# Six layer norms over features: sums as columns of tokens and a root on 128x2, instead of sums and root on all partitions

## Chip, cores, metric

One core of a Trainium2 chip runs the whole program. The metric is device time in microseconds of one execution, over several runs.

## What is computed

Two layers of a diffusion backbone with 256 latent tokens and 256 context tokens of 1024 features. Each layer mixes tokens (long convolution, attention, pooling), projects, adds a residual and normalises; then a SwiGLU feed-forward follows, again with a residual and a norm. The norm is the part that this change is about:

```python
def layer_norm(x, g, b):
    xf = x.astype(jnp.float32)
    mu = jnp.mean(xf, axis=-1, keepdims=True)
    var = jnp.mean(jnp.square(xf - mu), axis=-1, keepdims=True)
    return ((xf - mu) * lax.rsqrt(var + EPS) * g + b).astype(x.dtype)
...
    xl = layer_norm(DN_ALPHA * xl + g1_l * stream_mixer(pl, ql, k_all, v_all, lp), lp['ln1_g'], lp['ln1_b'])
    xl = layer_norm(DN_ALPHA * xl + g2_l * swiglu(xl * (1 + sc2_l) + sh2_l, lp), lp['ln2_g'], lp['ln2_b'])

    if not last:
        qc = queries(pc, lp['q_norm_g'])
        xc = layer_norm(DN_ALPHA * xc + g1_c * stream_mixer(pc, qc, kc, vc, lp), lp['ln1_g'], lp['ln1_b'])
        xc = layer_norm(DN_ALPHA * xc + g2_c * swiglu(xc * (1 + sc2_c) + sh2_c, lp), lp['ln2_g'], lp['ln2_b'])
```

Layer 0 normalises both streams, latent and context, twice; layer 1 only the latent one. That makes six norms of 256 tokens each.

## The kernel before

Features lie on the partitions: x is 128 partitions by 8 tiles (KT) by tokens, 512 of them in layer 0 (stream 0 is the first 256, stream 1 the second) and 256 in layer 1. Weights are fetched in blocks of 128x1024 by DMAs on SP's queue (`wblock`), split by ACT into a rounded high part (`whi`, L162) and by DVE into the rest (`wlo`, L159), and every product is three matmuls on PE: high by high, high by low, low by high (L169, L170, L171; or L273 where `dense_by_feature` goes over the features in the outer loop, so that a feature tile of the input can be used as soon as it is there). Results of dense blocks go to three PSUM buffers (`mm`); norms and other small things share five more (`aux`). The tile framework gives every engine a list of instructions in an order that its scheduler sets from priorities; `high_priority` moves what stands in it ahead of other work. Each engine then takes its own list strictly in turn. Generators in `self.bg` are advanced a step at a time by `pump`, between tiles of a dense block.

A norm has four parts. `ln_start` (L867) takes a 128x512 buffer `lnacc`. `ln_tile` (L873, L879) is called for each of the eight feature tiles when its projection is in PSUM: L884 on DVE adds the gated projection to the residual in x (and so frees the PSUM buffer), L890 on ACT squares it into `lnq`, L894 and L895 add value and square to `lnacc`; the last tile's are left out of that. `ln_sums` (L897) multiplies `lnacc` with a 128x128 matrix of 1/1024, `self.ones`, which puts the sums over the 128 features of every token on all partitions of a PSUM tile, `lnbc` (L900). `ln_finish` (L902, L915) adds the last feature tile and its square to it in the same way (L922), so that `lnbc` holds mean and mean square of each token, the same on every partition. ACT squares the mean (L924), DVE makes the variance (L925) and a reciprocal root in two steps by `newton` (L286: L290, L297, L298, L300, L301) on 128x256, into `lnrm`; ACT copies the mean beside it (L927). Then, for feature tiles 0, 1 and pairs (2,3), (4,5), (6,7), DVE subtracts the mean (L932) and multiplies by the root (L933), and ACT and DVE make the next stage's operands (`h2` or `h`: L939, L944, L159) or the output (L947, L949, with an output DMA of each pair on SP, L1175).

What stands around the six norms:

- Layer 0, first norms. The last five tiles of the output projection `wo` are made for stream 0 and then, with the same five weight blocks, for stream 1 (L1144 to L1148). Stream 0's finish goes to `bg` and runs during stream 1's tiles. Behind them come the first blocks of the feed-forward, `f` (L169 on `h2h` for stream 0, L273 for stream 1).
- Layer 0, second norms. Both finishes give layer 1's input `h`; behind them come layer 1's first projections, `u` (three blocks by feature, L273) and `q`.
- Layer 1, first norm. Five blocks `f` are computed from the sum before it is normalised (`raw`, L273), and `from_raw` (L974: L977, L979, L980) corrects them with mean and root into `fraw`; the other blocks read the normalised `h` (L169).
- Layer 1, second norm: the end of the program.

Elsewhere, the column form exists already: `hfss` (L420) sums over partitions by matmuls with one column of `ones`, and `hfrs` takes the root on 128x2; `newton` has a branch for that shape (L294, one instruction for each column). `bcast_cols` (L317, L322, L323) multiplies the identity by a column on DVE and lets PE multiply that diagonal matrix by `ones`, which puts the column on all partitions as a row; it is used for the attention's keys (`krb`).

## Time and profile before

| | |
|---|---|
| median of three runs | 1701.2 us (1699.5 to 1703.41) |
| profiled execution | 1701.23 us |
| its span | 1699.4 us |
| granted TensorE clock, mean of the span | 0.993 |
| PE, PEld, DVE, ACT, POOL busy | 97%, 85%, 72%, 42%, 13% of the span |
| HBM | 141 GB/s over the span |

The span runs from the first instruction to the last. PE stands for matmuls, PEld for the loads of their stationary operand, which overlap with them. A busy share is an average over the program; the wait lists and timelines say what is late at one place.

### The profile page before, as it was taken

The numbers are of one execution on the slowest core, as the hardware profiler recorded it, in microseconds if no ns is written. First come the engines' busy times: TensorE is split into PE (matmuls) and PEld (weight loads), VectorE is DVE, ScalarE is ACT, GpSimd is POOL, SyncE is SP. The second block draws the span as 40 slices with busy tenths as digits, with TensorE's granted clock in tenths as the row PEclk, the third lists the DMA queues.
The fourth block names the chain that finished last, engine by engine and source line by source line (L and its number), as shares of the span: only waits on it lengthen the run. The fifth ranks groups of instructions, "written<-read, shape, count | busy, mean of one in ns | idle before, by whom it ended". The sixth has DMA issues, their size and how long they took to land.

```text
span 1699.4 us, 25553 instructions
## 1 busy us (share of the span) xinstructions
PE 1650.9 (97%) x9926; PEld 1443.3 (85%) x9926; DVE 1227.5 (72%) x2145; ACT 710.3 (42%) x1138; POOL 219.9 (13%) x169
## 2 busy tenths in 40 slices
PE   7999999999999999999999999999989899999996
PEld 1888878788888888988888888899989899989996
DVE  4688879755677775789876567498767986796655
ACT  2533332533454433442222222275425664564443
POOL 1134541000210000000000012113531100000000
PEclk9999999999999999999999999999999999999998
DMA  8422222453422344226666664144426435645552
GB/s 307 168 88 87 66 84 79 152 161 124 137 75 90 113 159 136 100 82 201 189 199 196 205 197 151 62 159 140 152 92 186 125 118 169 196 140 186 185 185 91
DMA packets 68897, 243.34 MB, mean 143 GB/s; under 512 B 8166, under 2 KB 8744, under 8 KB 68520
## 3 DMA queue, kind: packets, MB, share of 16 engines
q1 hardware_dynamic: 67192, 236.78, 42.8%
q0 software_dynamic: 1168, 4.72, 0.9%
q8 instruction: 78, 1.28, 0.3%
q10 hardware_dynamic: 416, 0.21, 0.1%
q14 instruction: 43, 0.35, 0.1%
HBM read 238.01 MB, written 1.05 MB: 141 GB/s over the span
## 4 chain that ended last, share of the span: by engine, by line
PE 84%; DVE 10%; ACT 3%; issue 2%; DMA 1%; POOL 0%; ACTq 0%; DVEq 0%; POOLq 0%
PE f L169 6%; PE f L171 6%; PE f L170 6%; PE g L169 4%; PE g L171 4%; PE g L170 4%; PE b L169 4%; PE b L171 4%; PE b L170 4%; PE w L169 4%; PE w L171 3%; PE w L170 3%; PE ux L169 2%; PE ux L170 2%; DVE wlo L159 2%
## 5 line engine op out<-in xcount | busy, mean ns | idle before, releaser
L162 ACT ACTIVATE whi<-raw 128x1024 fp32r<-128x1024 f32 x322 | 340.6, 1059 | 679.9 <-issue 203.6
L159 DVE TENSOR_TENSOR wlo<-raw,whi 128x1024 fp32r<-128x1024 f32 x310 | 402.9, 1301 | 199.4 <-ACT whi L162 196.6
L190 DVE SCALAR_TENSOR_TENSOR junk<-ada,silu 128x1024 bf16<-128x1024 f32 x128 | 158.7, 1241 | 39.3 <-DMA ada<-adat 38.5
L169 PE MATMUL f<-h2h,whi 128*128 128x512 f32 (+1 forms) x320 | 125.1, 391 | 0.1
L170 PE MATMUL f<-h2l,whi 128*128 128x512 f32 (+1 forms) x320 | 124.5, 389 | 0.0
L171 PE MATMUL f<-h2h,wlo 128*128 128x512 f32 (+1 forms) x320 | 124.5, 389 | 0.0
L169 PE MATMUL f<-h,whi 128*128 128x256 f32 x312 | 88.4, 283 | 1.7 <-DVE fraw L979 1.6
L169 PE MATMUL w<-a,whi 128*128 128x256 f32 (+1 forms) x284 | 90.1, 317 | 0.0
L170 PE MATMUL w<-a,whi 128*128 128x256 f32 (+1 forms) x284 | 89.3, 314 | 0.0
L171 PE MATMUL w<-a,wlo 128*128 128x256 f32 (+1 forms) x284 | 89.2, 314 | 0.0
L171 PE MATMUL f<-h,wlo 128*128 128x256 f32 x312 | 87.6, 281 | 0.6 <-DVE wlo L159 0.6
L170 PE MATMUL f<-h,whi 128*128 128x256 f32 x312 | 88.1, 282 | 0.0
L169 PE MATMUL g<-hh,whi 128*128 128x512 f32 x192 | 75.6, 394 | 0.0
L171 PE MATMUL g<-hh,wlo 128*128 128x512 f32 x192 | 75.4, 393 | 0.0
L170 PE MATMUL g<-hl,whi 128*128 128x512 f32 x192 | 75.3, 392 | 0.0
L169 PEld LDWEIGHTS f<-h2h,whi 128*128 128x128 f32 x320 | 60.0, 188 | 14.1 <-DVE sg L1022 0.9
L171 PEld LDWEIGHTS f<-h2h,wlo 128*128 128x128 f32 x320 | 60.1, 188 | 13.6
L170 PEld LDWEIGHTS f<-h2l,whi 128*128 128x128 f32 x320 | 60.1, 188 | 13.1
L169 PEld LDWEIGHTS f<-h,whi 128*128 128x128 f32 x312 | 58.4, 187 | 2.3 <-issue 1.9
L171 PEld LDWEIGHTS f<-h,wlo 128*128 128x128 f32 x312 | 59.2, 190 | 0.8 <-DVE wlo L159 0.8
L170 PEld LDWEIGHTS f<-h,whi 128*128 128x128 f32 x312 | 58.6, 188 | 0.0
L169 PEld LDWEIGHTS w<-a,whi 128*128 128x128 f32 x284 | 53.5, 188 | 3.9 <-issue 0.2
(483 smaller groups left out, 4789.1 us busy)
## 6 DMA issues: line engine op xcount, KB each, us to landing
raw<-wst SPq DMA_DIRECT2D x336, 512.0 KB, 3.5
ada<-adat SPq DMA_DIRECT2D x80, 512.0 KB, 3.8
adar<-ada SPq DMA_DIRECT2D x16, 512.0 KB, 9.5
x<-x_t POOLq DMA_DIRECT2D x1, 2048.0 KB, 9.7
x<-x_t SPq DMA_DIRECT2D x1, 1024.0 KB, 10.5
x<-x_t SPq DMA_DIRECT2D x2, 512.0 KB, 10.2
silu<-c_row SPq DMA_DIRECT2D x2, 512.0 KB, 7.4
wf<-hfw SPq DMA_DIRECT2D x4, 256.0 KB, 5.8
```

The source lines that it names most:

```text
L159: (eng or self.nc.vector).tensor_tensor(out=lo, in0=src, in1=hi.bitcast(F32), op=ALU.subtract)
L162: self.nc.scalar.activation(hi, src, AF.Copy)
L169: t.matmul(out, lhsT=ah, rhs=bh, start=start, stop=False)
L170: t.matmul(out, lhsT=ah, rhs=bl, start=False, stop=False)
L171: t.matmul(out, lhsT=al, rhs=bh, start=False, stop=stop)
L190: nc.vector.scalar_tensor_tensor(out=junk, in0=raw, scalar=1.0, in1=self.silu[:, s], op0=ALU.mult, op1=ALU.mult, accum_out=mod[:, s, m : m ...
```

## The change

The six norms get another form. In `ln_sums`, the tokens become the rows: `lnacc`, 128 tokens of it at a time, is the stationary operand and one column of `ones` the moving one, so each matmul gives the sums of 128 tokens as a column of 128 partitions (`lnst`, a PSUM tile of its own: two for the values, two for the squares); DVE copies these four columns (L902). In `ln_finish`, four more such matmuls give the last feature tile's sums (L908 for all eight), L930 adds the copy, and mean, variance and root are computed on 128x2 (L935, L936, `newton` with its branch for two columns). `bcast_cols` puts the mean, and after it the root, on all partitions, each by two diagonal matrices and two matmuls of 128 columns (L322, L323), into one PSUM tile `lnrb`; the diagonals are multiplied by 1024, since `ones` holds 1/1024. In layer 0 ACT copies both from PSUM to `lnrm` (L943); in layer 1 DVE reads them in PSUM (`keep`), and the first norm there makes the copies for `from_raw` as well. Subtraction and multiplication are L949 and L950. At the call for the first norm of each layer, the finish's priority `pf` goes from 0 to 100.

The diff:

```diff
--- before.py
+++ after.py
@@ -314,12 +314,12 @@
         nc.vector.tensor_scalar(out=a, in0=a, scalar1=PI_LO, scalar2=-PI_LO, op0=ALU.min, op1=ALU.max)
         nc.scalar.activation(out, a, AF.Sin)
 
-    def bcast_cols(self, ps_out, cols):
+    def bcast_cols(self, ps_out, cols, scale=1.0):
 
         nc = self.nc
         for i in range(cols.shape[1]):
             dg = self.sb.tile([P, P], F32, tag="diag", name=self.nm("diag"), bufs=2)
-            nc.vector.tensor_scalar_mul(dg, self.ident, cols[:, i : i + 1])
+            nc.vector.tensor_scalar(out=dg, in0=self.ident, scalar1=cols[:, i : i + 1], scalar2=float(scale), op0=ALU.mult, op1=ALU.mult)
             nc.tensor.matmul(ps_out[:, i * P : (i + 1) * P], lhsT=self.ones, rhs=dg, start=True, stop=True)
 
 
@@ -864,9 +864,9 @@
                 nc.vector.scalar_tensor_tensor(out=x, in0=x, scalar=scale, in1=cb, op0=ALU.mult, op1=ALU.subtract)
             yield
 
-    def ln_start(self, y, s, g, pt, pf):
+    def ln_start(self, y, s, g, pt, pf, keep):
         ts = slice(s * SEQ, (s + 1) * SEQ)
-        st = dict(y=y[:, :, ts], g=g[:, s], s=s, pt=pt, pf=pf)
+        st = dict(y=y[:, :, ts], g=g[:, s], s=s, pt=pt, pf=pf, keep=keep)
         st["acc"] = self.t2b(shape=[P, 2, SEQ], name="lnacc")
         return st
 
@@ -896,8 +896,16 @@
 
     def ln_sums(self, st):
 
-        bc = st["bc"] = self.aux([P, 2, SEQ], name="lnbc")
-        self.nc.tensor.matmul(bc, lhsT=self.ones, rhs=st["acc"], start=True, stop=False)
+        st["bc"] = self.aux(name="lnst")
+        self.ln_columns(st, (st["acc"][:, 0], st["acc"][:, 1]), 0)
+        st["c"] = self.small([P, 4], "lnc4")
+        self.nc.vector.tensor_copy(st["c"], st["bc"][:, 0:4])
+
+    def ln_columns(self, st, srcs, o):
+        for i, src in enumerate(srcs):
+            for j in range(2):
+                k = o + 2 * i + j
+                self.nc.tensor.matmul(st["bc"][:, k : k + 1], lhsT=src[:, j * P : (j + 1) * P], rhs=self.ones[:, 0:1], start=True, stop=True)
 
     def ln_finish(self, st, *a, **k):
         g = self.ln_finish_(st, *a, **k)
@@ -917,14 +925,23 @@
         nc = self.nc
         y, s = st["y"], st["s"]
         ts = slice(s * SEQ, (s + 1) * SEQ)
-        bc, a, t = st["bc"], st["acc"][:, 0], st["acc"][:, 1]
-        for i, src in enumerate((y[:, KT - 1], st["sq"])):
-            nc.tensor.matmul(bc[:, i], lhsT=self.ones, rhs=src, start=False, stop=i == 1)
-        rm = st["rm"] = self.t2b(shape=[P, 2, SEQ], name="lnrm")
-        nc.scalar.activation(t, bc[:, 0], AF.Square)
-        nc.vector.scalar_tensor_tensor(out=a, in0=bc[:, 1], scalar=EPS, in1=t, op0=ALU.add, op1=ALU.subtract)
-        self.newton(rm[:, 0], a, t)
-        nc.scalar.activation(rm[:, 1], bc[:, 0], AF.Copy)
+        self.ln_columns(st, (y[:, KT - 1], st["sq"]), 4)
+        c = st["c"]
+        nc.vector.tensor_tensor(out=c, in0=st["bc"][:, 4:8], in1=c, op=ALU.add)
+        rb = self.aux([P, 2, SEQ], name="lnrb")
+        self.bcast_cols(rb[:, 1], c[:, 0:2], D)
+        w = self.small([P, 4], "lnw")
+        a, t = w[:, 0:2], w[:, 2:4]
+        nc.vector.tensor_tensor(out=t, in0=c[:, 0:2], in1=c[:, 0:2], op=ALU.mult)
+        nc.vector.scalar_tensor_tensor(out=a, in0=c[:, 2:4], scalar=EPS, in1=t, op0=ALU.add, op1=ALU.subtract)
+        self.newton(c[:, 2:4], a, t)
+        self.bcast_cols(rb[:, 0], c[:, 2:4], D)
+        rm = rb
+        if "raw" in st or not st["keep"]:
+            st["rm"] = self.t2b(shape=[P, 2, SEQ], name="lnrm")
+            for i in (1, 0):
+                nc.scalar.activation(st["rm"][:, i], rb[:, i], AF.Copy)
+            rm = rb if st["keep"] else st["rm"]
         yield
         for i in range(0, KT, 2):
             for m, n in ((i, 1), (i + 1, 1)) if i == 0 else ((i, 2),):
@@ -1130,7 +1147,7 @@
         al = self.scaled(self.v(l, V_LN1G, 8), self.v(l, V_LN1B, 8))
         fo = [self.fold(self.v(l, V_LN1G, 8), self.v(l, V_LN1B, 8), mod[4][:, s], mod[3][:, s]) for s in range(ns)]
         raw = self.raw_pair(*fo[0]) if ns == 1 else None
-        lns = [self.ln_start(y, s, mod[2], (20, 50)[l], 0) for s in range(ns)]
+        lns = [self.ln_start(y, s, mod[2], (20, 50)[l], 100, last) for s in range(ns)]
         if raw:
             lns[0]["raw"] = raw, fo[0][0]
         for m in range(KT - nb):
@@ -1167,7 +1184,7 @@
         g, b = self.v(l, V_LN2G, 8), self.v(l, V_LN2B, 8)
 
         def start():
-            return [self.ln_start(y, s, mod[5], 0, (100, 0)[l]) for s in range(ns)]
+            return [self.ln_start(y, s, mod[5], 0, (100, 0)[l], last) for s in range(ns)]
 
         if last:
             def finish(s, st):
```

How the lists of instructions move is shown at two places. The names after L-number and operation are output, inputs and shape; `x` is the residual that becomes the normalised value, `h2l` and `h` the low part of the next stage's operand.

DVE, layer 0, first norms, before: the part of the list around L884 of stream 1's second `wo` tile (`wo_5878`).

```order
L925 SCALAR_TENSOR_TENSOR lnacc_5539<-lnbc_5811,lnacc_5539 128x256
L290 TENSOR_SCALAR lnrm_5866<-lnacc_5539 128x256
L297 TENSOR_TENSOR lnacc_5539<-lnrm_5866 128x256
L932 TENSOR_TENSOR x_4920<-x_4920,lnrm_5866 128x256
L298 TENSOR_TENSOR lnacc_5539<-lnacc_5539 128x256
L884 SCALAR_TENSOR_TENSOR x_4920<-wo_5878,mod_73,x_4920 128x256
L300 SCALAR_TENSOR_TENSOR lnacc_5539<-lnacc_5539 128x256
L894 TENSOR_TENSOR lnacc_5540<-lnacc_5540,x_4920 128x256
L301 SCALAR_TENSOR_TENSOR lnrm_5866<-lnacc_5539,lnrm_5866 128x256
L895 TENSOR_TENSOR lnacc_5540<-lnacc_5540,lnq_5904 128x256
L297 TENSOR_TENSOR lnacc_5539<-lnrm_5866 128x256
```

DVE at the same place in the change: from L930 to the same L884 (here `wo_5901`), in two pieces.

```order
L930 TENSOR_TENSOR lnc_1019_5816<-lnst_5811,lnc_1019_5816 128x4
L322 TENSOR_SCALAR diag_5875<-ident,lnc_1019_5816 128x128
L322 TENSOR_SCALAR diag_5878<-ident,lnc_1019_5816 128x128
L935 TENSOR_TENSOR lnw_5881<-lnc_1019_5816 128x2
L936 SCALAR_TENSOR_TENSOR lnw_5881<-lnc_1019_5816,lnw_5881 128x2
L290 TENSOR_SCALAR lnc_1019_5816<-lnw_5881 128x2
L294 SCALAR_TENSOR_TENSOR lnw_5881<-lnc_1019_5816,lnw_5881 128x1 x2
L300 SCALAR_TENSOR_TENSOR lnw_5881<-lnw_5881 128x2
L301 SCALAR_TENSOR_TENSOR lnc_1019_5816<-lnw_5881,lnc_1019_5816 128x2
L294 SCALAR_TENSOR_TENSOR lnw_5881<-lnc_1019_5816,lnw_5881 128x1 x2
L301 SCALAR_TENSOR_TENSOR lnc_1019_5816<-lnw_5881,lnc_1019_5816 128x2
```

```order
L159 TENSOR_TENSOR h2l_5659<-lnt_6016,h2h_5658 128x256
L961 TENSOR_SCALAR lnt_6020<-x_4920,fold_5531 128x256
L895 TENSOR_TENSOR lnacc_5540<-lnacc_5540,lnq_5865 128x256
L159 TENSOR_TENSOR h2l_5659<-lnt_6020,h2h_5658 128x256
L949 TENSOR_TENSOR x_4920<-x_4920,lnrm_5898 128x2x256
L884 SCALAR_TENSOR_TENSOR x_4920<-wo_5901,mod_73,x_4920 128x256
```

Before, this L884 is the fifth row behind L925. Now 33 rows of the list stand between L930 and it, three quarters of stream 0's finish among them.

DVE, second norm of layer 0, stream 0, before: the end of the root, and two splits of weights for `u` (`wlo_9104`, `wlo_9110`).

```order
L932 TENSOR_TENSOR x_4920<-x_4920,lnrm_8980 128x2x256
L298 TENSOR_TENSOR lnacc_7936<-lnacc_7936 128x256
L159 TENSOR_TENSOR wlo_9104<-raw_9101,whi_9103 128x1024
L301 SCALAR_TENSOR_TENSOR lnrm_8980<-lnacc_7936,lnrm_8980 128x256
L159 TENSOR_TENSOR wlo_9110<-raw_9107,whi_9109 128x1024
L933 SCALAR_TENSOR_TENSOR x_4920<-x_4920,lnrm_8980 128x256 x2
L944 TENSOR_SCALAR lnt_9009<-x_4920,fold_8959 128x256
```

DVE at the same place in the change: the first split of weights ahead of the subtraction, and the two others at the end of the norm (`u_9193` is the first product of `u` that DVE reads).

```order
L322 TENSOR_SCALAR diag_9052<-ident,lnc_1514_8986 128x128
L322 TENSOR_SCALAR diag_9055<-ident,lnc_1514_8986 128x128
L159 TENSOR_TENSOR wlo_9178<-raw_9175,whi_9177 128x1024
L949 TENSOR_TENSOR x_4920<-x_4920,lnrm_9058 128x256 x2
```

```order
L961 TENSOR_SCALAR lnt_9158<-x_4920,fold_9010 128x256
L159 TENSOR_TENSOR h_9009<-lnt_9154,h_9009 128x256
L159 TENSOR_TENSOR h_9009<-lnt_9158,h_9009 128x256
L159 TENSOR_TENSOR wlo_9184<-raw_9181,whi_9183 128x1024
L159 TENSOR_TENSOR wlo_9190<-raw_9187,whi_9189 128x1024
L547 SCALAR_TENSOR_TENSOR vv_9279<-u_9193,vecs,vv_9279 128x255
```

Two splits stood ahead of the first multiplication and the third behind the last `h`; now one stands ahead of it and two behind the last `h`. In PE's list, 46 rows of the second and third `u` products stand behind these two splits.

## Rows read from the trace of the kernel before

**Rows 1.** Page, part 1: busy time, share of the span, instructions of each engine.

```profile
PE 1650.9 (97%) x9926; PEld 1443.3 (85%) x9926; DVE 1227.5 (72%) x2145; ACT 710.3 (42%) x1138; POOL 219.9 (13%) x169
```

**Rows 2.** Waits of PE: us in total, times, longest us.

```profile
PE f L273 <- ACT h2h L939: 2.1, 1, 2.1
...
PE u L273 <- ACT h L939: 1.7, 1, 1.7
PE f L169 <- DVE fraw L979: 1.6, 1, 1.6
PE lnbc L900 <- DVE lnacc L895: 1.3, 1, 1.3
```

**Rows 3.** Timeline of PE: start us, duration us, engine, line, out<-in.

```profile
706.36 0.59 PE L922 MATMUL lnbc<-x,ones 128*128 128x256 f32 x2
...
707.33 0.28 PE L170 MATMUL wo<-mh,whi 128*128 128x256 f32 x1
707.45 0.28 PE L171 MATMUL wo<-mh,wlo 128*128 128x256 f32 x1
...
718.40 0.28 PE L169 MATMUL f<-h2h,wx 128*128 128x256 f32 x1
...
1121.76 0.28 PE L169 MATMUL q<-h,whi 128*128 128x256 f32 x1
```

**Rows 4.** Timeline, all engines: a column sum, then a root on 128x2.

```profile
76.71 0.40 PE L171 MATMUL ux<-hh,wlo 128*128 128x512 f32 x1
...
76.94 0.50 PE L420 MATMUL hfss<-ones,wf 128*128 128x1 f32 x4
...
77.48 0.16 DVE L423 TENSOR_SCALAR hfrs<-hfss 128x2 f32<-128x2 f32 x1 [2.33 <-PE hfss L420]
77.62 0.40 PE L170 MATMUL uv<-hl,whi 128*128 128x512 f32 x1
...
77.88 0.35 DVE L294 SCALAR_TENSOR_TENSOR hfrs<-hfrs 128x1 f32<-128x1 f32 x2
```

**Rows 5.** Timeline, all engines: diagonal matrices and their broadcast.

```profile
1245.68 0.51 DVE L322 TENSOR_SCALAR diag<-ident,krs 128x128 f32<-128x128 f32 x2 [0.45 <-PE krb L323]
...
1246.03 0.71 PE L323 MATMUL krb<-diag,ones 128*128 128x128 f32 x4
...
1246.70 0.28 PE L170 MATMUL v<-wlo,h 128*128 128x256 f32 x1
...
1246.78 0.69 DVE L710 SCALAR_TENSOR_TENSOR kf<-kf,krb 128x512 f32<-128x512 f32 x1 [0.58 <-PE krb L323]
```

**Rows 6.** Timeline of DVE, first norms of layer 0.

```profile
710.80 0.48 DVE L884 SCALAR_TENSOR_TENSOR x<-wo,mod,x 128x256 f32<-128x256 f32 x1
```

**Rows 7.** Timeline of DVE, second norm of layer 0, stream 0.

```profile
1109.20 0.75 DVE L933 SCALAR_TENSOR_TENSOR x<-x,lnrm 128x256 f32<-128x256 f32 x2
...
1110.86 0.69 DVE L933 SCALAR_TENSOR_TENSOR x<-x,lnrm 128x512 f32<-128x512 f32 x1
1111.46 0.42 DVE L159 TENSOR_TENSOR h<-lnt,h 128x256 fp32r<-128x256 f32 x1
...
1117.34 1.21 DVE L159 TENSOR_TENSOR wlo<-raw,whi 128x1024 fp32r<-128x1024 f32 x1
```

**Rows 8.** Stretch there: busy share of each engine, then PEclk, DMA share, GB/s.

```profile
1112.00:1115.00 3.00, 3.00 (x14) 3.00 (x15) 3.00 (x9) 3.00 (x7) 0.00 (x0) 0.50 0.77 292
```

**Rows 9.** Timeline of DVE, layer 1, first norm.

```profile
1491.58 0.42 DVE L925 SCALAR_TENSOR_TENSOR lnacc<-lnbc,lnacc 128x256 f32<-128x256 f32 x1
...
1500.01 0.76 DVE L933 SCALAR_TENSOR_TENSOR x<-x,lnrm 128x256 f32<-128x256 f32 x2
...
1506.46 0.86 DVE L979 SCALAR_TENSOR_TENSOR fraw<-lnrm,rawc,f 128x256 f32<-128x256 f32 x2
```

**Rows 10.** Timeline of DVE, last norm.

```profile
1686.45 0.42 DVE L925 SCALAR_TENSOR_TENSOR lnacc<-lnbc,lnacc 128x256 f32<-128x256 f32 x1 [1.72 <-ACT lnacc L924]
...
1692.30 1.96 DVE L933 SCALAR_TENSOR_TENSOR x<-x,lnrm 128x256 f32<-128x256 f32 x4
```


## The prediction

> **What bounds the kernel now.** I read the page first: PE is busy in 97% of the span [rows 1], so time is lost in two ways only, by giving PE more to do or by letting it stand. The next view is what PE waits for. At the six norms it stands 2.1 us before the by-feature matmuls of stream 1 of layer 0 (L273 on h2h), 1.7 us before the first matmul of layer 1 (L273 on h) and 1.6 us before the first dense block behind layer 1's first norm (L169 on fraw) [rows 2]. These are the places where a norm is the chain that ends last, with the end of the program as the fourth: behind the last norm there is no PE work left to cover it. The timelines of PE and DVE at these places give the prices, and the two order listings say what each queue holds behind what. The sum stands against the profiled execution, 1701.23 us (span 1699.4); the median of the three runs shown is 1701.2, so the two agree. A measurement of this kernel can tell about 0.2%, 3.4 us, from no change.
>
> **PE's work per norm.** Removed: one ones-matmul over 512 columns and two over 256. From 706.36 to 707.33 stand the two narrow ones and one wo matmul, whose pitch is 0.12 (707.33 to 707.45), so 0.85 [rows 3]. The wide one has as many columns as both: 1.7 in all. Added: eight matmuls with one column and four of 128 columns. Two single-column matmuls (four records) and one matmul of 512 columns, whose pitch is 0.23 (76.71 to 76.94), take 76.94 to 77.62, so 0.45 for two [rows 4]; eight make 1.8. Two broadcasts with a diagonal matrix (four records) and one v matmul of 0.12 lie between 1246.03 and 1246.70, so at most 0.55; I take 0.45, because that is the price of four such records in rows 4 and the load sets both [rows 5]. Four make 0.9. So **PE gets 2.7 in place of 1.7, +1.0 us a norm**; ends: +0.7 (if a wide ones-matmul costs 0.3 more than two narrow ones) and +1.2 (0.55 for each pair).
>
> **DVE's work per norm.** Removed: L925 and eight root steps on 128x256, with five subtractions 5.85 us from L925 to the first multiply in the last norm [rows 10]. The subtractions there are two of 256 and three of 512 columns. In a row, 256 columns take 0.34 (0.75 for two, less one of 0.42) and 512 take 0.60 (1110.86 to 1111.46) [rows 7], so 2.5 us, and the nine steps take 3.4. Added: a copy and an addition on 128x4, ten steps on 128x2, four diagonal matrices. Two steps go from 77.48 to 77.88, 0.20 each, and a pair of L294 with its hand-over takes 0.39 [rows 4]; ten make 2.0. Two diagonal matrices take 0.51, start to end [rows 5], about 0.4 to 0.5 in a row. Sum 3.4: DVE saves nothing. What changes is the shape. Before, the mean was on all partitions first and the five subtractions filled the gaps between root steps. Now mean and root share a PSUM tile, the first subtraction (L949) stands behind both pairs of diagonals in DVE's queue, and all subtractions are on the path behind the root.
>
> The price of 128x2 deserves a check. A step on 128x256 takes 0.42 [rows 10] and one on 128x2 takes 0.16 with a pitch of 0.20 [rows 4]: with 1/128 of the elements, more than a third of the time. [...] The trace's own 0.20 is what I use.
>
> **Chain from sums to first subtraction.** L930 0.2, two diagonals 0.4, L935 and L936 0.4, the root 1.65, two diagonals 0.4, and 0.6 from there to the reader (the idle 0.58 before L710 in rows 5): 3.65 us.
>
> **Layer 0, first norms: +2.9.** The change also raises the finish's priority from 0 to 100. In the after order all of stream 0's finish but its tail stands ahead of stream 1's L884 on its second wo tile, which runs at 710.80 now [rows 6] while the root is still being made. Between L930 and that L884 stand 4 diagonals (1.0), 10 small steps (2.0), 19 operations of 256 columns at 0.34 (6.5), 5 of 512 at 0.6 (3.0) and one weight split (1.2, as in rows 7): 13.7 us. From about 706, where the last sums are on PE now [rows 3], that ends at 719.7. Stream 1 has three mm buffers; its last wo tile needs the one that this L884 frees. PE would be there at 718.40 (first f matmul [rows 3]) less 24 matmuls of 0.12, plus 1.0: 716.5. It waits 3.2, and f starts at 722.6 and not 718.40. Then stream 1's own norm adds 1.0 less what the shorter queue behind it gives back (0.2), and its 2.1 us wait [rows 2] goes, since its finish then has more time: 4.2 + 0.8 - 2.1 = +2.9. Ends: 0 (the L884 slips in early enough) and +5.
>
> **Layer 0, second norms: +3.4.** The first multiply is at 1109.20 and PE's wait ends with it [rows 2, 7]. Now one weight split of 1.2 less stands ahead of it, and against that stand the columns, the two broadcasts' hand-overs and the subtractions: u starts within 0.3 of today. But the splits of the second and third u blocks stand behind all of h. One of them runs at 1117.34 now [rows 7], the other before the multiplies. In the after order, 46 PE rows stand behind them, at 0.12 a row 5.5 us. With h done at about 1117.4 and one split of 1.2 they can begin at 1118.6, so q starts at 1124.1 where it starts at 1121.76 [rows 3]: +2.3. Stream 1's broadcasts and hand-over add 1.1, since PE is full there. Ends: +1.1 (the splits get through) and +4.9 (half clock, below).
>
> **Layer 1, first norm: +2.8.** L925 runs at 1491.58, the first multiply, with all five subtractions done, at 1500.01, and fraw starts at 1506.46 [rows 9]. Now a weight split stands ahead of L930, so 1492.55; 3.65 for the chain and two splits of 1.2 inside it give the first subtraction at 1498.6. From there 2.5 for subtractions and the same 6.45 as today, plus up to 0.06 on each of ten operations that now read PSUM (L884, which does, takes 0.48 [rows 6], against 0.42): 1508.2, +1.8. The fourth dense block also waits for a buffer that the first fraw tiles free, behind copies (L994) that now stand together: +1 more, by the queue's rows. Ends: 0 (h's pieces come as early as now) and +4.3 (half clock).
>
> **Last norm: +0.5.** L925 starts at 1686.45 and waits for one activation behind the sums, so they are there at about 1686.0; plus 3.65 the first subtraction is at 1689.7; 2.5 of subtractions bring it to 1692.2, level with the 1692.30 of now [rows 10]. Ten operations that read PSUM cost 0.06 each more. Ends: -0.7 (first outputs leave earlier, and the last with them) and +1.
>
> **Sum:** 2.9 + 3.4 + 2.8 + 0.5 = +9.6 on 1701.2, so **1711**. PE's own +5 (five norms) is inside: where PE stands anyway it costs nothing. On ACT a square and a copy go and two copies come (layer 0): level. One early weight load moves later on SP's queue; the weights of that stretch are read many tiles later, so nothing, and a wait for it would show as PE on whi. A norm holds two PSUM aux buffers of five, not one; no wait for one is among rows 2, so nothing, at worst a tile's 0.5.
>
> **Rivals.**
> *Faster.* [...] 0.13.
> *Same.* The new waits fall on the old ones: stream 1's L884 is done by about 717, so that PE stands under 1 us there and the 2.1 goes (+0.5 in all), and both u splits are through by 1118 (only stream 1's +1.1 stays), and the fourth dense block's +1 is all that layer 1's first norm adds; with the last norm's +0.5 that is +3.1, 1704, and down to 1700 if PE's added work lies in waits everywhere. For it: three of the four terms rest on a place in a queue, not on work. Against: each has to fall well. 0.19.
> *Slower still.* New idle stretches of 2 to 3 us at three places halve the clock again, as 1.73 us of standing came before the 0.50 of rows 8: 1.5 each, 1714 to 1715.5. 0.13. For it: that row; against: in the 2.1 us before stream 1's L273 DVE and ACT do what now shortens, so not every stretch need grow.
> *Cheap small steps.* [...] 0.05. [...]
>
> **How the numbers follow.** The forecast's own case, 1705 to 1714, has 0.50. Slower by over 0.2%: 0.50 + 0.13 + 0.05 = 0.68; within 0.2%: 0.19; faster: 0.13. The range 1698 to 1716 leaves out most of the faster case (0.1) and the top of the slower-still one (0.05).
>
> **What would show it.** Right: a PE wait of some 3 us on DVE x L884 in the last wo tile of layer 0; the wait of L273 on h2h gone; no wait at u's start above 2 but q late, about 1124 plus what came before; the first L949 of the end 3.6 us behind the sums; lnst matmuls 0.45 a pair. Wrong: PE's waits at the six norms smaller in sum than today's 6.7, or the small steps under 0.15 apart. If PE shows no L884 wait, the first term falls and the time is about 1708; if u's splits come before h, another 2.3 goes.

## The result and the profile after

The changed kernel takes 1714.91 us (median of 4 runs, 1712.82 to 1717.95) where the kernel before takes 1701.71 (4 runs, 1699.5 to 1703.41): a ratio of 1.0079, with an interval of 1.0065 to 1.0092. It is 13.2 us slower. The profiled execution took 1712.82 with a span of 1711.0, 11.6 us over the span of before.

The page of the changed kernel, part 1:

```profile
PE 1661.8 (97%) x10034; PEld 1458.4 (85%) x10034; DVE 1227.7 (72%) x2187; ACT 710.4 (42%) x1136; POOL 219.6 (13%) x169
```

PE's share is what it was, 97%, and DVE's busy time is the same to 0.2 us [rows 1]: no engine was relieved. PE has 10.9 us more of busy time, of which its own added work is only a part. Another part is the clock: behind the wait for fraw, f rows come 0.21 us apart until 1522 and 0.12 apart after that.

Waits of PE in the changed kernel (us in total, times, longest):

```profile
PE f L169 <- DVE fraw L996: 3.8, 1, 3.8
...
PE wo L169 <- DVE x L884: 2.5, 1, 2.5
...
PE u L273 <- DVE x L884: 1.3, 1, 1.3
...
PE u L273 <- ACT h L956: 0.7, 1, 0.7
```

The 2.1 us wait of L273 on h2h [rows 2] is gone, and the 1.7 us wait of u on h has shrunk to 0.7. In their place stand 2.5 us of the last wo tile on L884 and, inside u, 1.3 us on L884; the wait for fraw has grown from 1.6 to 3.8.

Timeline of PE, with the places of rows 3:

```profile
719.86 0.44 PE L169 MATMUL wo<-mh,wx 128*128 128x256 f32 x1 [2.48 <-DVE x L884]
...
724.34 0.28 PE L169 MATMUL f<-h2h,wx 128*128 128x256 f32 x1
...
728.77 0.50 PE L908 MATMUL lnst<-ones,x 128*128 128x1 f32 x4
...
729.58 0.36 PE L169 MATMUL f<-h2h,wx 128*128 128x256 f32 x1
...
741.22 0.63 PE L273 MATMUL f<-h2h,wx 128*128 128x256 f32 x4
...
1129.73 0.28 PE L169 MATMUL q<-h,whi 128*128 128x256 f32 x1
```

The first f row starts at 724.34 (718.40 before), stream 1's first L273 at 741.22, the first q row at 1129.73 (1121.76 before). Four column matmuls take 0.81 (728.77 to 729.58). DVE at the two ends of the piece of its list that PE waits for, and then at layer 0's second norm:

```profile
706.01 0.16 DVE L930 TENSOR_TENSOR lnc<-lnst,lnc 128x4 f32<-128x4 f32 x1 [1.50 <-PE lnst L908]
...
719.33 0.48 DVE L884 SCALAR_TENSOR_TENSOR x<-wo,mod,x 128x256 f32<-128x256 f32 x1
```

```profile
1120.70 0.75 DVE L159 TENSOR_TENSOR h<-lnt,h 128x256 fp32r<-128x256 f32 x2
1121.37 2.35 DVE L159 TENSOR_TENSOR wlo<-raw,whi 128x1024 fp32r<-128x1024 f32 x2
```

L884 of stream 1's second wo tile runs at 719.33 (710.80 before [rows 6]). At the second norm the last piece of h ends at 1121.45 and both late splits come behind it. DVE at layer 1's first norm and at the last norm:

```profile
1500.16 0.16 DVE L930 TENSOR_TENSOR lnc<-lnst,lnc 128x4 f32<-128x4 f32 x1 [0.97 <-PE lnst L908]
...
1507.02 0.42 DVE L949 TENSOR_TENSOR x<-x,lnrb 128x256 f32<-128x256 f32 x1 [1.73 <-ACT lnrm L943]
...
1516.66 0.86 DVE L996 SCALAR_TENSOR_TENSOR fraw<-lnrm,rawc,f 128x256 f32<-128x256 f32 x2
```

```profile
1695.44 0.48 DVE L884 SCALAR_TENSOR_TENSOR x<-w,mod,x 128x256 f32<-128x256 f32 x1 [2.07 <-PE w L171]
1697.13 0.16 DVE L930 TENSOR_TENSOR lnc<-lnst,lnc 128x4 f32<-128x4 f32 x1 [1.21 <-PE lnst L908]
...
1701.35 0.42 DVE L949 TENSOR_TENSOR x<-x,lnrb 128x256 f32<-128x256 f32 x1 [1.12 <-PE lnrb L323]
```

fraw starts at 1516.66 (1506.46 before [rows 9]); in the last norm the first subtraction comes 4.2 us behind L930. The granted clock in three stretches, in which PE had work all the time (PEclk is the third number from the end):

```profile
720.00:723.00 3.00, 3.00 (x15) 3.00 (x16) 3.00 (x9) 3.00 (x7) 0.00 (x0) 0.51 0.00 0
1123.00:1126.00 3.00, 3.00 (x16) 3.00 (x16) 2.96 (x7) 0.56 (x1) 0.00 (x0) 0.50 0.68 227
1519.00:1522.00 3.00, 3.00 (x16) 3.00 (x15) 2.60 (x6) 3.00 (x8) 0.00 (x0) 0.50 0.02 5
```

Half the clock (0.50 to 0.51), right behind the wait at 719.86, in the last part of u, and behind the wait for fraw. Each such stretch lasted some 3.4 us (the last one from 1518.8 to 1522.2), so PE does up to 1.7 us of work less in it, an estimate: half of 3.4. Before the last norm the span of before has four of them (at 282, 1112, 1163 and 1320), that of the change seven (at 221, 283, 720, 1122, 1273, 1327 and 1518).

To see where the time goes, each PE row of one trace was set against the same row of the other, and the difference of their starts read at fixed places. "Elsewhere" is what comes between the norms. "Stretches" counts those at half clock before the last norm; one of 7 us counts as two. For all kernels, against the profiled execution of before (us):

| kernel | layer 0, first norms | layer 0, second norms | layer 1, first norm | last norm | elsewhere | span | stretches |
|---|---|---|---|---|---|---|---|
| the change | +3.5 | +5.9 | +3.5 | +0.4 | -1.7 | +11.6 | 7 |
| prio_only | +3.9 | 0.0 | +6.1 | 0.0 | -1.4 | +8.6 | 9 |
| after_pf0 | +0.6 | +5.9 | +6.6 | +0.5 | -1.4 | +12.2 | 9 |
| after_two_tiles | +1.3 | +6.4 | +10.7 | +0.4 | -2.7 | +16.1 | 8 |
| after_two_tiles_pf0 | +5.6 | +6.1 | +3.7 | -0.1 | -0.3 | +15.0 | 9 |
| after_filler | +1.9 | +6.8 | +6.4 | +0.5 | -1.2 | +14.3 | 8 |
| after_u_splits | +3.5 | +8.7 | +6.0 | +0.4 | +0.4 | +19.0 | 10 |
| norms2_only | 0.0 | +7.5 | +0.3 | +0.5 | -3.5 | +4.8 | 4 |
| last_norm_only | 0.0 | +0.1 | +0.1 | +0.5 | -3.1 | -2.4 | 4 |
| before_filler | +1.5 | -0.2 | 0.0 | 0.0 | -1.1 | +0.2 | 5 |
| last_norm_ordered | 0.0 | -0.2 | 0.0 | -0.4 | 0.0 | -0.6 | 4 |
| norm1_layer1_only | 0.0 | -0.1 | +7.4 | 0.0 | -0.1 | +7.2 | 7 |
| after_two_fillers | +1.8 | +6.0 | +4.9 | +0.5 | -1.7 | +11.5 | 6 |

The columns of one place are the safer reading: the same edit gives much the same number there unless a stretch comes or goes. Where nothing was changed they show -0.2 to 0.3, but for the +1.5 of before_filler, which is a stretch at 737. The spans, one execution each, carry the clock of that execution. The changed kernel's loss at the norms is 3.5 + 5.9 + 3.5 + 0.4 = 13.3; of the 1.7 got back elsewhere, 1.6 is the stretch at 1163 that before's profiled execution had and this one had not.

The profiled execution of the change is the fastest of its four, so the clock of all executions matters too. The record gives each one's span and mean granted clock. The 77 executions of the kernel before that were measured beside the runs below are longer where the clock is lower: 1696.5 us in the mean at 0.994 (8 of them), 1703.9 at 0.988 (4). At the same clock the change is 8.9 to 10.2 us slower: 1711.0 against 1702.1 at 0.990, 1713.0 against 1702.9 at 0.989, 1713.2 against 1703.9 at 0.988, 1716.2 against 1706.0 (one execution) at 0.987. Its mean clock is 0.9885, that of the 77 is 0.9912. So 9 to 10 of the 13.2 us are lost at equal clock, and the rest goes with a lower one.

### The profile page after: what moved, and what is told of

Read it like the earlier page. It is cut to its first block, busy times and chain, and to the rows that moved or that the text cites. A ratio compares the mean times of both kernels' runs of the same rounds, so it can differ in the third digit from the quotient of the medians.

```text
span 1711.0 us, 25825 instructions
## 1 busy us (share of the span) xinstructions
PE 1661.8 (97%) x10034; PEld 1458.4 (85%) x10034; DVE 1227.7 (72%) x2187; ACT 710.4 (42%) x1136; POOL 219.6 (13%) x169
## 4 chain that ended last, share of the span: by engine, by line
PE 86%; DVE 8%; ACT 2%; issue 2%; DMA 1%; POOL 0%; ACTq 0%; DVEq 0%; POOLq 0%
PE f L169 7%; PE f L171 7%; PE f L170 6%; PE g L171 4%; PE g L169 4%; PE g L170 4%; PE b L169 4%; PE b L171 4%; PE b L170 4%; PE w L169 4%; PE w L171 4%; PE w L170 4%; PE ux L169 2%; PE ux L171 2%; PE ux L170 2%
## 5 line engine op out<-in xcount | busy, mean ns | idle before, releaser
L171 PEld LDWEIGHTS w<-a,wlo 128*128 128x128 f32 x284 | 53.4, 188 | 3.7
## 6 DMA issues: line engine op xcount, KB each, us to landing
adar<-ada SPq DMA_DIRECT2D x16, 512.0 KB, 10.2
x<-x_t SPq DMA_DIRECT2D x2, 512.0 KB, 10.2
```

Of the source, the lines that this page charges most:

```text
L171: t.matmul(out, lhsT=al, rhs=bh, start=False, stop=stop)
```

## The experiments

Each ratio is against executions of the kernel before that were measured beside that run; their medians lie between 1699.51 and 1702.89, so the ratio says more than the time.

**Priority alone.** The kernel before, with

```diff
-        lns = [self.ln_start(y, s, mod[2], (20, 50)[l], 0) for s in range(ns)]
+        lns = [self.ln_start(y, s, mod[2], (20, 50)[l], 100) for s in range(ns)]
```

> The kernel before with one edit: the finish of each layer's first norm at priority 100 and not 0. Theory (the priority puts stream 1's second L884 behind stream 0's finish, PE stands on the mm buffer): a wait of wo on DVE x L884 of 2 to 3 us, the 2.1 us wait of L273 on h2h gone, and a stretch at the half clock if the stand is long enough: 1703 to 1706. Rival (the form of the sums and of the root costs the time, the priority is harmless): within 1.5 us of before, no wait on L884.

Measured: 1708.97, ratio 1.004 (1.0027 to 1.0052). PE at the last wo tile, and the stretch behind it:

```profile
719.06 0.58 PE L169 MATMUL wo<-mh,wx 128*128 128x256 f32 x1 [3.46 <-DVE x L884]
```

```profile
718.00:725.00 7.00, 5.94 (x28) 5.95 (x29) 4.52 (x14) 4.43 (x9) 0.00 (x0) 0.53 0.01 2
```

The priority alone, with the old sums and the old root, makes the wait on L884 (3.46 us), with two stretches of half clock in the 7 us around its end, and costs layer 0's first norms 3.9, as much as the whole change does there. It costs another 6.1 at layer 1's first norm, which was not expected: PE stands 2.2 us there before L852 (at 1510.53, on ACT x), is at half clock for the next 6.6, and stands 2.1 more on sg at the fourth dense block; the wait for fraw is down to 0.7. So the time misses the expected 1703 to 1706. The rival is out for layer 0's first norms.

**The change with the priority back at 0.** The reverse edit on the changed kernel.

> The changed kernel with the priority of the first norms back at 0. Theory: L884 of stream 1 runs among the small steps again, the 2.5 us wait and the 1.7 us lost to the half clock behind it go; of the +3.9 at layer 0's first norms some +1 is left, so 1711 to 1712 where the change has 1714.9. Rival (the form): 1714 to 1716, the time lost at the by-feature matmuls in place of the wo tile.

Measured: 1713.08, ratio 1.0058 (1.004 to 1.0075). PE, the first L273 of stream 1:

```profile
738.36 0.63 PE L273 MATMUL f<-h2h,wx 128*128 128x256 f32 x4
```

738.36 where the change has 741.22 and the row before has 737.20, with no wait of wo. Layer 0's first norms fall to +0.6: the priority was nearly all of that term. But layer 1's first norm costs 6.6 here with three stretches, and the total moves less than expected: the interval overlaps that of the change (1.0065 to 1.0092).

**Two PSUM tiles.** The changed kernel, cut to the lines that matter:

```diff
-        rb = self.aux([P, 2, SEQ], name="lnrb")
-        self.bcast_cols(rb[:, 1], c[:, 0:2], D)
+        rbm = self.aux([P, SEQ], name="lnmb")
+        rb = self.aux([P, SEQ], name="lnrb")
+        self.bcast_cols(rbm, c[:, 0:2], D)
...
-        self.bcast_cols(rb[:, 0], c[:, 2:4], D)
+        self.bcast_cols(rb, c[:, 2:4], D)
```

> The changed kernel, priority 100 kept, with mean and root broadcast into a PSUM tile each, so that the subtractions depend on the mean alone and stand between the root's small steps in DVE's list. Theory (the subtractions moved behind the root lengthen the chain that PE or the end waits for): the last norm ends 1.5 to 2.5 us earlier, u and the first dense block behind fraw start 1 to 2 us earlier each: 1709 to 1712. Rival (the chain's length is hidden or set elsewhere, by queue places and by the clock): 1714 to 1716 with the last norm alone 1.5 shorter at most, 1713.

Measured: 1715.73, ratio 1.0073 (1.0056 to 1.0089); no gain. DVE in the last norm:

```profile
1699.95 0.48 DVE L884 SCALAR_TENSOR_TENSOR x<-w,mod,x 128x256 f32<-128x256 f32 x1 [2.08 <-PE w L171]
...
1703.45 0.42 DVE L951 TENSOR_TENSOR x<-x,lnmb 128x256 f32<-128x256 f32 x1 [0.66 <-PE lnmb L323]
...
1708.42 1.95 DVE L952 SCALAR_TENSOR_TENSOR x<-x,lnrb 128x256 f32<-128x256 f32 x4 [1.18 <-PE lnrb L323]
```

And the last L884 of the kernel before:

```profile
1684.25 0.48 DVE L884 SCALAR_TENSOR_TENSOR x<-w,mod,x 128x256 f32<-128x256 f32 x1 [6.37 <-PE w L171]
```

The subtractions did move in between the root's steps, but the first of them waits 0.66 for the mean's broadcast and holds up the root behind it, and DVE still stands 1.18 for the root's broadcast: from the last L884 (1699.95) to the end of the span (1715.5) it is 15.5 us, 15.6 in the change (1695.44 to 1711.0), 15.2 before (1684.25 to 1699.4). Here the subtractions that were put between the root's steps came to lie in the root's chain themselves. The expected gain fails at the last norm, and layer 1's first norm costs 10.7 here, with four stretches.

**Both edits.**

> Both edits: two PSUM tiles and priority 0 for the first norms. If the two causes are separate, their gains add: 1705 to 1709. If both cure the same wait, it is no better than the better of the two alone. Below 1701.7 only if the form itself, without its order, is a gain.

Measured: 1715.88, ratio 1.0071 (1.0052 to 1.0089). The gains don't add; layer 0's first norms are even at +5.6: PE stands 3.7 us for the diagonal matrices at 734 (L323 on DVE L322), with two stretches from 733 on.

**A filler on PE.** The changed kernel with matmuls whose result nobody reads, ahead of stream 1's last wo tile:

```diff
+                if s == ns - 1 and ns == 2 and i == nb - 1:
+                    z = self.aux(name="fillz")
+                    for _ in range(20):
+                        self.nc.tensor.matmul(z[:, :SEQ], lhsT=ws[i - 1][0][:, 0:P], rhs=mh[0][0][:, s * SEQ : (s + 1) * SEQ], start=True, stop=True)
                 o = self.mm(name="wo")[:, :SEQ]
```

> The changed kernel with 20 more matmuls of 256 columns on PE (some 2.4 us, their result is not read) ahead of the last wo tile of layer 0, where PE stands 2.5 us for L884 and its granted clock is 0.50 for 3.4 us after that. Theory (the stand brings the clock down, and the 1.7 us lost are part of the change's cost): the wait on L884 shrinks to near 0 at the same end, no half-clock stretch follows at 720, layer 0's first norms cost 1.8 and not 3.5 over before, 1713 in all. Rival (the clock falls there for another reason, or the matmuls come on top): the stretch stays, or the time grows by up to 2.4, 1715 to 1717.

Measured: 1716.86, ratio 1.0076 (1.0061 to 1.009). PE, and the clock where the change has 0.51:

```profile
717.10 2.43 PE L1165 MATMUL fillz<-mh,wx 128*128 128x256 f32 x20
...
722.47 0.36 PE L169 MATMUL f<-h2h,wx 128*128 128x256 f32 x1 [0.22 <-ACT x L975]
```

```profile
720.00:723.00 3.00, 2.78 (x24) 2.61 (x24) 3.00 (x10) 3.00 (x6) 0.00 (x0) 1.00 0.00 0
```

PE is busy for the time that it stood, the clock stays at 1.00, and f starts at 722.47 and not at 724.34. Layer 0's first norms cost 1.9 and not 3.5: 1.6 of the loss there was the half clock. The total is no better: the profiled execution has two stretches more at the norms behind (+6.8 and +6.4 there), and the mean clock of its six executions, 0.9885, is that of the change. That part of the expectation fails.

**The u splits ahead.** The changed kernel with

```diff
-            ws = [self.wblock(2 - i) for i in range(3)]
+            with self.tc.high_priority(300):
+                ws = [self.wblock(2 - i) for i in range(3)]
```

> The changed kernel with the fetch and the splits of the three u blocks of layer 1 at priority 300: in DVE's list they stand between the pieces of h and no longer behind all of h. Theory (46 PE rows behind two late splits are most of the +5.9 at layer 0's second norms): q starts 2 to 4 us earlier against the start of that stage, 1711 to 1713. Rival (the columns, broadcasts and hand-overs make that stage longer, the splits only fill its tail): h comes 2.4 later for it and the stage stays at +5 to +7, 1714 to 1716.

Measured: 1719.86, ratio 1.0093 (1.0077 to 1.0109): slower still. PE at q, and DVE at the end of h:

```profile
1129.56 0.36 PE L169 MATMUL q<-h,whi 128*128 128x256 f32 x1 [1.84 <-DVE vv L549]
```

```profile
1123.14 0.41 DVE L159 TENSOR_TENSOR h<-lnt,h 128x256 fp32r<-128x256 f32 x1
1127.75 0.16 DVE L930 TENSOR_TENSOR lnc<-lnst,lnc 128x4 f32<-128x4 f32 x1 [4.20 <-PE lnst L908]
```

The splits stand between the pieces of h now, and h ends at 1123.55, 2.1 later than in the change (0.2 of it came with it). DVE then stands 4.20 us at L930 of stream 1, whose columns PE has behind its u rows, and the rows that free u's PSUM buffers (L547, L549) stand behind that L930; q waits 1.84 for one of them. q starts 0.4 earlier against the start of the stage than in the change, where 2 to 4 was expected, though the change has a stretch ahead of q and this kernel none. The stage costs 8.7 and not 5.9, with two stretches from 1130 on. So the two late splits are not a loss that this earlier place gives back: there they delay h. My theory falls in that form.

**The second norms alone.** Both forms in one kernel, a flag for each norm; here the new one at the second norms of both layers, priority 0 at the first. The edit, cut to the flag:

```diff
+        if st["col"]:
+            return self.ln_sums_c(st)
...
-        g = self.ln_finish_(st, *a, **k)
+        g = (self.ln_finish_c if st["col"] else self.ln_finish_)(st, *a, **k)
```

> The new form at the second norms alone (layer 0 both streams, and the last norm); the first norms as before, priority 0. Theory (the terms are separate by place): +5.9 at layer 0's second norms and +0.5 at the end, 1707 to 1709 against before's 1701.7. Rival (a stage's loss depends on what the norm ahead of it did, or is clock by chance): under +3.

Measured: 1708.53, ratio 1.0029 (1.0017 to 1.0042). Layer 0's second norms cost 7.5 with two stretches, and 5.9 to 6.0 in the three kernels that have the new form there as it is and one stretch: this loss belongs to the form at that place, whatever the norms ahead do.

**The last norm alone.** The same kernel, the flag at the last norm only.

> The new form at the last norm alone. Theory (the shorter root and the subtractions behind it cancel): +0.5 us, 1702.2, not to be told from before; the span behind the last L884 0.3 to 0.7 longer than before's. Rival (the form is a gain where nothing else is in the queues): 1 to 2 us less.

Measured: 1701.56, ratio 0.9992 (0.9979 to 1.0005). DVE, the last L884:

```profile
1681.40 0.48 DVE L884 SCALAR_TENSOR_TENSOR x<-w,mod,x 128x256 f32<-128x256 f32 x1 [2.07 <-PE w L171]
```

The span ends at 1697.0, 15.6 us behind it; before 15.2. So +0.4 to +0.5, as expected, and not to be told from before in the time.

**A filler in the kernel before.** Fourteen matmuls ahead of u:

```diff
+            z = self.aux(name="fillz")
+            for _ in range(14):
+                self.nc.tensor.matmul(z[:, :SEQ], lhsT=ws[0][0][:, :P], rhs=ws[0][0][:, :SEQ], start=True, stop=True)
             self.dense_by_feature(ws, [o for _, o in self.early], h, 0, T)
```

> The kernel before with 14 matmuls of 256 columns on PE (1.7 us, result not read) between the last w tile and the first u matmul of layer 1, where PE stands 1.73 us and the granted clock is 0.50 from 1112 to 1115. Theory (standing brings the clock down): the stretch at 1112 goes, q starts 1.7 us earlier, 1700 and not 1701.7; elsewhere the same stretches come and go as between any two runs. Rival (the clock falls there for other reasons, such as the load on the DMAs, or it had no effect since h sets the pace): the stretch stays, or goes and q starts at the same time; 1701.7 to 1703.

Measured: 1700.99, ratio 0.9994 (0.9984 to 1.0005). PE, and the clock where before has 0.50 [rows 8]:

```profile
1110.47 1.84 PE L1072 MATMUL fillz<-whi 128*128 128x256 f32 x14
...
1123.60 0.28 PE L169 MATMUL q<-h,whi 128*128 128x256 f32 x1
```

```profile
1112.00:1116.00 4.00, 3.94 (x26) 3.16 (x25) 4.00 (x11) 4.00 (x9) 0.00 (x0) 1.00 0.91 281
```

The stretch is gone, and q starts at the same place: 1123.60 is 1.84 over before's 1121.76 [rows 3], and the rows ahead of this stage were already 2.0 late. The pieces of h set the pace there, so half the clock cost nothing.

**The last norm in another order.** The same filler, the new form at the last norm alone, two tiles, and the subtraction made to need the end of the root (against the changed kernel, cut to these lines):

```diff
+        one = self.small([P, 1], "one")
+        nc.vector.tensor_scalar(out=one, in0=c[:, 3:4], scalar1=0.0, scalar2=1.0, op0=ALU.mult, op1=ALU.add)
...
-                nc.vector.tensor_tensor(out=yn, in0=yn, in1=rm[:, 1:2].to_broadcast([P, n, SEQ]), op=ALU.subtract)
+                nc.vector.scalar_tensor_tensor(out=yn, in0=yn, scalar=one[:, 0:1], in1=mean.to_broadcast([P, n, SEQ]), op0=ALU.mult, op1=ALU.subtract)
```

> The kernel before with the same filler, and the new form at the last norm alone with two edits: mean and root in a PSUM tile each, and the subtractions tied to the end of the root (a factor of 1 made behind it), so that DVE makes the diagonals of the root first and then subtracts while PE broadcasts. Theory (of the 1.12 us that DVE stands for the root's broadcast, two subtractions of 0.34 fill a part): from the last L884 to the last output activation 0.5 to 0.7 shorter than with the new form as it was, so level with before or 0.2 better; with the filler 1699.5 to 1700.5. Rival (the hand-over is not the limit, the output DMAs are): the end comes at the same distance as in last_norm_only.

Measured: 1701.56, ratio 0.9998 (0.9987 to 1.0009). DVE in the last norm:

```profile
1684.12 0.48 DVE L884 SCALAR_TENSOR_TENSOR x<-w,mod,x 128x256 f32<-128x256 f32 x1 [2.07 <-PE w L171]
...
1688.42 0.48 DVE L322 TENSOR_SCALAR diag<-ident,lnc 128x128 f32<-128x128 f32 x2
...
1689.01 0.87 DVE L1001 SCALAR_TENSOR_TENSOR x<-x,one,lnmb 128x256 f32<-128x256 f32 x2
1689.96 0.75 DVE L1002 SCALAR_TENSOR_TENSOR x<-x,lnrb 128x256 f32<-128x256 f32 x2
```

The diagonals of the root come first, two subtractions fill the time in which PE broadcasts, and DVE stands no more: from the last L884 to the end of the span (1698.8) it is 14.7 us, 0.9 less than in the form as it was and 0.5 less than before. The order was the cost in this norm, not the form. In the time of the whole kernel 0.5 us can't be told from nothing; no version here is faster than the kernel before by more than its interval.

**Layer 1's first norm alone.** The flag at that norm, priority 0.

> The new form at the first norm of layer 1 alone, priority 0. Theory (the form costs this place +1.8 by itself, from the small steps' order around the weight splits and the subtractions behind the root, and the rest of the change's +3.5 there is a half-clock stretch behind the 3.75 us wait): fraw's wait 3.5 to 4, 1703.5 to 1705.5 with one or two stretches at 0.50 behind it. Rival (the loss there comes from the priority or from what the norms ahead did): under +1 with a wait near before's 1.6.

Measured: 1707.91, ratio 1.0032 (1.0016 to 1.0048). PE at the columns and at the first dense f row:

```profile
1489.94 0.61 PE L974 MATMUL lnst<-ones,lnacc 128*128 128x1 f32 x4 [3.19 <-DVE lnacc L894]
...
1513.02 0.36 PE L169 MATMUL f<-h,whi 128*128 128x256 f32 x1 [3.78 <-DVE fraw L1051]
```

The wait for fraw is 3.78, as in the change, and the wait ahead of the columns 3.19 (1.3 before [rows 2]); two stretches at half clock follow them (the 18 raw rows from 1491.50 to 1494.87 come 0.19 apart in the mean, the f rows from 1514.73 to 1517.72 0.21, and 0.12 ahead of that). The wait for fraw came as expected, but the place costs 7.4, more than the 1.8 and one or two stretches of 1.7 that were expected, and more than the change's 3.5; the time is above the expected 1703.5 to 1705.5. Neither theory nor rival had the longer wait ahead of the columns. The new form costs time at this place by itself, without the priority and with the norms ahead as before.

**Two fillers.** The filler at wo, and thirty matmuls ahead of layer 1's first dense f block (the second, cut):

```diff
+                if l and len(us) == 1 and f < 3 and not self.early:
+                    w = self.wblock()
+                    z = self.aux(name="fillz")
+                    for _ in range(30):
+                        self.nc.tensor.matmul(z[:, :SEQ], lhsT=w[0][:, :P], rhs=w[0][:, :SEQ], start=True, stop=True)
```

> The changed kernel with the 20 extra matmuls ahead of layer 0's last wo tile and 30 more (3.5 us) ahead of layer 1's first dense f block behind the raw head, where PE stands 3.75 us for fraw. Theory (standing brings the clock down, and where PE sets the pace afterwards, as at both places, that time is lost): no half-clock stretch at 720 nor behind 1517, layer 0's first norms again +1.85, layer 1's first norm 1.7 less than with a stretch, so about +2 over before: 1711 to 1713. Rival (the extra matmuls delay f, or the stretches only move to the next places where PE stands): 1714 to 1717.

Measured: 1713.71, ratio 1.0078 (1.0057 to 1.0099). PE in layer 1, and the clock behind both places where it stood:

```profile
1494.71 0.61 PE L908 MATMUL lnst<-ones,lnacc 128*128 128x1 f32 x4 [1.63 <-DVE lnacc L894]
...
1513.40 3.76 PE L1030 MATMUL fillz<-whi 128*128 128x256 f32 x30
...
1517.76 0.36 PE L169 MATMUL f<-h,whi 128*128 128x256 f32 x1 [0.17 <-DVE fraw L996]
```

```profile
1495.00:1498.00 3.00, 3.00 (x19) 3.00 (x20) 3.00 (x5) 1.98 (x4) 0.00 (x0) 0.65 0.61 188
1518.00:1521.00 3.00, 3.00 (x27) 3.00 (x27) 2.40 (x11) 3.00 (x7) 0.00 (x0) 1.00 0.00 0
```

No stretch at 720, nor behind the first dense f row: 1518 to 1521 has 1.00. But another one has come up at 1495, behind the 1.63 us wait of the columns, fraw starts 4.6 late against the start of the place (2.5 in the change), and the place costs 4.9. The rival's second half holds there: the stretch moved. The ratio is that of the change (1.0079).

## Why the prediction was right, and where it was not

**Direction and size.** The forecast was +9.6, and +13.2 came. 1714.91 is inside the range, but above the forecast's own case (1705 to 1714) and in the band of the rival "slower still" (1714 to 1715.5). Both had a part in it: the losses came at the places of the forecast, and three new stretches at half clock (at 720, 1122 and 1518) lie behind them. The sum of the places, 13.3, is 3.7 over the forecast's; less 1.7 for each of the three stretches it is 8.2, an estimate, since only the first was taken away by a run (1.6, after_filler). At equal clock whole executions give 8.9 to 10.2. That 9.6 lies so near is in part luck: by the same estimate the first and third terms were each 1 us too large and the second 0.8 too small.

**Layer 0, first norms: +2.9 forecast, +3.5 measured.** The wait was where it was forecast, on L884 of stream 1's second wo tile (2.48 us for 3.2), and L273's wait on h2h went. prio_only and after_pf0 show that the priority makes it. The term was mis-sized in two parts that partly cancel: without the stretch behind the wait the place costs 1.8 to 1.9 (after_filler, after_two_fillers), not 2.9, and the stretch adds 1.6.

**Layer 0, second norms: +3.4 forecast, +5.9 measured**, beyond the upper end of +4.9. q starts 8.0 late, of which 3.9 came with it: +4.1 where 2.3 was forecast. Stream 1's part makes the other 1.8 (1.1 forecast). u's start was forecast within 0.3 us, and it is at 1114.68, 0.4 over the shift ahead of it; h ends at 1121.45, as forecast (1117.4 and the 3.9 that came with it). What the sum lacked is the clock: the half-clock stretch lies on the last u rows (0.50 from 1123 to 1126), through which PE has no wait, and in before it lay where it costs nothing (before_filler). That the two late splits are the cause was argued from the order; after_u_splits shows that moving them ahead gains little at q and nothing in the stage. Which of DVE's rows sets that stage's length stays open; norms2_only shows only that the form does it at this place.

**Layer 1, first norm: +2.8 forecast, +3.5 measured.** fraw starts 10.2 late, of which 7.7 came with it: +2.5 where 1.8 was forecast. The first subtraction comes 6.9 us behind L930 (1500.16 to 1507.02), where 6.05 was forecast: DVE stands 1.73 ahead of it, behind ACT's copies of mean and root, where 0.6 was put in. The fourth dense block's wait on sg is 0.5, where 1 was forecast. The term holds in the main, with a stretch on top. But it isn't the form's alone: priority with the old form costs 6.1 there, the new form without the priority 6.6 and 7.4, both together 3.5 to 6.4. Losses at this place don't add, and no run shows why.

**Last norm: +0.5 forecast, +0.4 measured**, and +0.5 alone. That was luck, since the working was off inside in two parts that cancel. The chain from L930 to the first subtraction is 4.2 and not 3.65, since DVE stands 1.12 for the hand-over and not 0.58; the granted clock is 0.50 there from 1700 to 1702. Against that, the subtraction that reads PSUM takes 0.42 (L949 at 1701.35), as a step on 128x256 that doesn't [rows 10], so the 0.06 on each of ten operations did not come.

**The prices.** Four columns took 0.81 (0.9 forecast); the loads for L908 and L323 are much alike (191 and 201 ns in the mean, `lnst<-ones,lnacc` and `lnrb`). No run shows cheap small steps, which have 0.05 in the sum of chances: the root's come 0.20 apart in the last norm too (L936 at 1697.91, L290 at 1698.11), where under 0.15 would have spoken against the forecast. What PE's +1.0 a norm cost no run shows by itself.

**The rival "faster"**, 0.13 in the sum of chances, is shown by no run. The half-clock stretch at 1112 [rows 8] went in before_filler, and nothing was gained by it. Of the four waits of rows 2 one went, one shrank to 0.7, the 1.3 on lnacc came out at 1.1, and the one for fraw grew to 3.8.

**The fillers.** With PE busy in place of standing, the clock stayed at 1.00 at all three places: from 720 to 723 in after_filler, from 1112 to 1116 in before_filler, from 1518 to 1521 in after_two_fillers, where it was 0.50 to 0.51 before or in the change. In after_filler and after_two_fillers stretches came elsewhere, and the ratio of the whole kernel stayed where it was.

## What to carry to other kernels

Where PE stands in a kernel that PE bounds (97% busy here), look whether a stretch at half clock follows as a second loss, as it did behind 1.73 us at u's start in the kernel before and behind 2.48 us at wo and 3.75 us at fraw in the change, and ask whether PE or its suppliers set the pace there: it cost 1.6 us behind the wo tile, and nothing at u's start in the kernel before. The priority moved more here than the work it was set on (3.9 us at layer 0's first norms in prio_only): look up which row, that frees a buffer or feeds another engine, ends up behind it. And where a chain of tiny steps ends in a hand-over to another engine, put work that doesn't need the result behind its last step, into the hand-over, and not between its steps: in the last norm that was 14.7 us against 15.5.

## What had not been expected of the hardware

Waits of nearly the same length (1.87 and 1.86 us, 2.83 and 2.86 us) were followed by half the clock in one execution and not in another. Two PE rows in the kernel before, with the clock behind them:

```profile
1161.65 0.39 PE L171 MATMUL q<-h,wlo 128*128 128x256 f32 x1 [1.87 <-DVE wlo L159]
...
1263.97 0.39 PE L171 MATMUL up<-h,wlo 128*128 128x256 f32 x1 [2.83 <-DVE wlo L159]
```

```profile
1163.00:1166.00 3.00, 3.00 (x17) 3.00 (x17) 2.93 (x5) 0.65 (x1) 2.21 (x2) 0.53 0.88 324
1266.00:1269.00 3.00, 2.62 (x24) 2.43 (x22) 3.00 (x2) 0.00 (x0) 3.00 (x2) 1.00 0.37 111
```

The first row again in last_norm_only, where the norms ahead of it are as before, with the clock behind it:

```profile
1162.14 0.39 PE L171 MATMUL q<-h,wlo 128*128 128x256 f32 x1 [1.86 <-DVE wlo L159]
```

```profile
1163.00:1166.00 3.00, 3.00 (x27) 3.00 (x27) 2.93 (x6) 0.32 (x1) 1.72 (x2) 1.00 0.87 258
```

And the second row in the change:

```profile
1272.09 0.39 PE L171 MATMUL up<-h,wlo 128*128 128x256 f32 x1 [2.86 <-DVE wlo L159]
```

```profile
1273.00:1276.00 3.00, 3.00 (x16) 3.00 (x15) 3.00 (x3) 0.00 (x0) 3.00 (x3) 0.50 0.49 175
```

Behind q's wait of 1.87 the clock falls in before (0.53), and behind 1.86 it stays in last_norm_only; behind up's wait of 2.83 it stays in before, and behind 2.86 it falls in the change (0.50). So here a wait of 1.9 to 2.9 us was followed by a stretch or not, and each is worth up to 1.7 us by the estimate above. That is why one execution's span says little about an edit of 2 us here, and why the columns by place were needed.
